# Moving the code for an expert's third to eighth token tile behind all experts

## The chip, the cores and the metric

The kernel runs on one core of one Trainium2 chip. The metric is the device time of one execution in microseconds (us); lower is better. The time before is the median of three runs.

## The reference

One layer of a diffusion backbone over 1024 latent tokens of width 1024 (and 256 context tokens), all float32: a modulated projection, neighbourhood attention beside a gated token MLP, an output projection, and then a mixture of experts. The change touches the experts alone:

```python
p_g = softmax(t @ rg_w + rg_b); p_top, g_idx = top_k(p_g, 1)          # 1 of 4 groups
e_top, e_idx = top_k(softmax(logits of that group's 4 experts), 2)     # 2 of 4 experts
gate = p_top * e_top / sum(e_top)                                      # spread to 16 columns
for e in range(16):
    hid = silu(t @ w1[e]) * (t @ w3[e])        # 1024 -> 512
    out = out + gate[:, e:e+1] * (hid @ w2[e]) # 512 -> 1024
```

Each token has two of the 16 experts, so the 16 counts of tokens add up to 2048; one expert may have anything from none to 1024 of them. The counts are known only when the program runs.

## The kernel before, in words

Projections, attention, output projection and router take the first 600 us; the router writes lists of the tokens of each expert to memory. The experts follow, in a written order (a manual schedule: every engine runs its instructions in the order of the source). Tokens of an expert are taken in tiles of 128 (`P`). A product in float32 is made of three matmuls of rounded parts (`mm3`, lines 86 to 88): high by high, high by low, low by high. Each matmul is two instructions of TensorE's stream, the load of the stationary operand (PEld in the profile) and the matmul (PE).

The weights of an expert are six chunks of 1 MB. A chunk is loaded into one of seven `raw` slots by the SP queue (`e_load`, lines 922 and 925), and is split by `e_conv` into a rounded part `chi` (ScalarE, line 941) and a rest `clo` (VectorE or GpSimd, line 946); when the rest of chunk g is made, the load of chunk g+7 is issued. So weights are loaded a little over one expert ahead.

For expert e, TensorE does the first half of the hidden columns of its first tile (`h_mm(e, 0, 0)`), then the further tiles (`more1(e)`), then the rest of the first tile: the second half (`h_mm(e, 0, 1)`), the transposes of the hidden values (`h_T`), the transposes of the next expert's first tile (`x_split`), and the second product (`y_mm`). `y_out` multiplies by gate and scatters the rows into `out` with an accumulating DMA of the GpSimd queue.

The further tiles stand under `tc.If` on `cr[e]`, the expert's count, a register that each of the five engines loads. An `If` is a compare-and-branch in the stream of each engine. `more1` (line 1521) asks whether there is a second tile at all; `second` (line 1467) takes `one` for a tile of more than 64 tokens (76 matmuls for a second tile) or `other` for a smaller one (52 matmuls, both parts in one stationary operand). Within `one` stands `more(e, 2)` (line 1504), which holds the third tile, and nested in it the fourth to the eighth. Expert 0 has only its first two tiles in place; what it has beyond them stands behind all experts (line 1583), where its weights are loaded once more.

Of the kernel before, what the change touches and what calls it, by code (L numbers as in the profile page):

```python
# [11 lines left out]
F32 = mybir.dt.float32  # L12
F32R = mybir.dt.float32r
BF16 = mybir.dt.bfloat16
I32 = mybir.dt.int32
AF = mybir.ActivationFunctionType
ALU = mybir.AluOpType
AX = mybir.AxisListType.X
# [3 lines left out]
P = 128  # L22
# [6 lines left out]
E = 16  # L29
# [10 lines left out]
def hybrid_layer_kernel(ctx, tc, a, out):  # L40
    nc = tc.nc
# [22 lines left out]
    cst = ctx.enter_context(pool("cst"))  # L64
# [22 lines left out]
        nc.tensor.matmul(po, xh, wl, start=False, stop=False)  # L87
        nc.tensor.matmul(po, xl, wh, start=False, stop=last)  # L88

# [1 line left out]
    es_p1 = ExitStack()  # L91
    p1 = es_p1.enter_context(pool("p1", side="right"))
    hp = es_p1.enter_context(pool("hp", side="right"))
# [86 lines left out]
        nc.sync.dma_start(xt, src)  # L180
        xts[t] = xt

    # rows (shift, 1 + scale) for c and c_ctx, each on all partitions
    ada = [[xp.tile([P, D], F32, name=f"ada{c}{v}") for v in range(2)] for c in range(2)]
    hT = {t: tuple(hp.tile([P, KD, P], F32R, name=f"{n}{t}") for n in ("hhi", "hlo")) for t in range(NT)}
    sqs = {}
# [62 lines left out]
            if sk == 6:  # L249
                nc.tensor.matmul(pas[j], onesr[0:2, :], bAr[j], start=False, stop=False)  # L250

    # the bias rows as a rounded part and the rest of it, on two partitions
    def bias_split():
        for v, hf in blocks:
            b = bA[:, v * D + hf * 512:v * D + hf * 512 + 512]
# [44 lines left out]
            es_w.close()  # L300
            hcp.append(es_hc.enter_context(pool("hcp", side="right")))

    # rows of a token tile where positions of a chunk come first and chunks second
    def by_pos(d, t):
        aa, b = divmod(t, 4)
        return _ap(d, (b * 256 + aa * 4) * 512, [[8 * 512, 32], [512, 4], [1, 512]])

    # rows of a token tile in the order of the keys: row group, column group, place
    def by_key(d, t, i):
        aa, b = divmod(t, 4)  # L310
        return _ap(d, (aa * 512 + b * 64) * D + i * 512, [[D, 64], [256 * D, 2], [1, 512]])
# [99 lines left out]
        return first  # L411

    def gelu_parts(t, x):
        # gelu from tanh, which is in the table set of exp
        g = gl[0]

        def p1_():
            nc.scalar.activation(g, x, AF.Square)
            nc.gpsimd.tensor_scalar(g, g, 0.044715, 1.0, op0=ALU.mult, op1=ALU.add)

        def p2_():
            nc.vector.tensor_tensor(g, g, x, op=ALU.mult)
            nc.scalar.activation(g, g, AF.Tanh, scale=math.sqrt(2.0 / math.pi))

        def p3_():
            nc.vector.scalar_tensor_tensor(g, g, 1.0, x, op0=ALU.add, op1=ALU.mult)

        m = mixt.pop(t)
        r = at0.tile([P, 1], F32, name="ru")

        def p4_():
            nc.gpsimd.tensor_scalar(g, g, 0.5, None, op0=ALU.mult)
            nc.gpsimd.tensor_tensor(g, g, m, op=ALU.mult)

        def p5_():
            nc.scalar.activation(m, g, AF.Square, accum_out=r)
            nc.gpsimd.tensor_tensor(g, g, og[1], op=ALU.mult)

        def p6_():
            rsqrt(r, r, 1.0 / 512, EPS)  # L440
            nc.gpsimd.tensor_tensor(g, g, r.to_broadcast([P, 512]), op=ALU.mult)
            nc.gpsimd.dma_start(yD[t * P:(t + 1) * P, 512:1024], g)

        def skip():
            pass
        tails.extend([p1_, p2_, p3_, p4_, skip, skip, p5_, skip, p6_])
# [38 lines left out]
            if f == 1:  # L485
                es_m.close()

    # gate and shift / scale rows of the second part, summed over the contraction on DVE
    rowD = dram.tile([4, D], F32, name="rowD")
    ada_loads = [(v, k) for v in range(4) for k in range(KD)]  # L490
    ada_raw, splits, sums = [], [], []
# [100 lines left out]
    for g, (nm, c0) in enumerate(GROUPS):  # L592
        tiles = list(range(NT))
        if nm == "v":
            tiles = tiles + [8, 9]
        if nm == "k":
            tiles = [8, 9] + tiles
        if nm == "k":
            knp.append(es_kn.enter_context(pool("knp")))
        for it, t in enumerate(tiles):  # L600
            last = it == len(tiles) - 1
# [51 lines left out]
            for k in range(KD):  # L653
# [12 lines left out]
                if k == 6:  # L666
                    if splits:
                        v = splits.pop()
# [29 lines left out]
            KS = kvp.tile([P, H, 1280], F32R, name="KS")  # L698
    es_p1.close()

# [1 line left out]
    es_o = ExitStack()  # L702
    gfp = ctx.enter_context(pool("gfp", side="right"))
    gf2 = gfp.tile([P, 2, D], F32, name="gf2")
# [5 lines left out]
    op = es_o.enter_context(pool("op", side="right"))  # L710
# [13 lines left out]
    at = es_a.enter_context(pool("at"))  # L724
# [44 lines left out]
        for lo, tr, hi in w:  # L769
            nc.vector.tensor_tensor(lo, tr, hi.bitcast(F32), op=ALU.subtract)  # L770

    # The rounded parts and the rests of v and of the weights are both side by side:
    # one pass gives all four products, which are added up on the way to o.
    def pv(t, h):
        pt = PTs.pop((t, h))
        o = psc.tile([P, 512], F32, tag="OT", name="OT").rearrange("p (a q) -> p a q", a=4)[:, 0:2]
# [113 lines left out]
    es_a0.close()  # L890
    es_kv.close()

# [1 line left out]
    g_a, sh_f, sc_f, g_f = bc  # L894
    NS, NR = 6, 7
    CH = 6 * E
# [4 lines left out]
    raw = [rawp.tile([P, 2048], F32, name=f"raw{i}") for i in range(3)]  # L901
# [4 lines left out]
    chi = [sl0.tile([P, 2048], F32R, name=f"chi{i}") for i in range(2)]  # L906
# [12 lines left out]
    def w_chunk(e, c, r, eng):  # L919
        if c < 4:  # L920
            for i, w in enumerate(("w1", "w3")):
                eng.dma_start(r.rearrange("p (k n) -> p k n", k=4)[:, :, i * 256:(i + 1) * 256],
                                  a[w][e, (c % 2) * 512:(c % 2) * 512 + 512, (c // 2) * 256:(c // 2) * 256 + 256].rearrange("(k p) n -> p k n", p=P))
        else:
            eng.dma_start(r.rearrange("p (k n) -> p k n", k=2),
                              a["w2"][e, (c - 4) * 256:(c - 4) * 256 + 256, :].rearrange("(k p) n -> p k n", p=P))
# [132 lines left out]
        nc.vector.tensor_scalar(eq, eq, f, None, op0=ALU.is_equal)  # L1059
        return m, eq  # L1060

    # one operation at a time; names mark the ends of its parts
    def route(t):
        pl = pls[t][1]
        lg = sm([P, 20], "lg")
# [28 lines left out]
        yield "pr"  # L1094
        nc.vector.tensor_tensor(msum, msum, mb, op=ALU.add)
        if t >= NT - 2:
            # places of this tile's tokens among the first tokens of expert 0
            key = sm([P, 1], "key")
            nc.vector.scalar_tensor_tensor(key, pr[:, 0:1], 1.0, mb[:, 0:1], op0=ALU.add, op1=ALU.mult)
            sel0[t] = sm([P, P], "sel0")  # L1100
            nc.vector.tensor_scalar(sel0[t], iota, key, None, op0=ALU.is_equal)
            yield "sel"
        # gates: p_top / (1 + ex) and that times ex
        ng = sm([P, 1], "ng")
        nc.vector.tensor_scalar(ng, gm, -1.0, None, op0=ALU.mult)
        nm1 = sm([P, 1], "nm1")
# [5 lines left out]
        ex = sm([P, 1], "ex")  # L1112
# [25 lines left out]
        den = sm([P, 1], "den")  # L1138
        nc.vector.scalar_tensor_tensor(den, ex, 1.0, zg, op0=ALU.add, op1=ALU.mult)
        yield  # L1140
        # the second list holds the token as a difference to the first list's row for no token
        dl = sm([P, 2, 2], "dl", I32)
        dlf = dl.bitcast(F32)
        nc.vector.reciprocal(dlf[:, 0, 1:2], den)
# [42 lines left out]
        if t + 2 < NT:  # L1187
            y_load(t + 2)

    # The first tokens of expert 0: those of all tiles but two are gathered here,  # L1190
    # those of the last two join by a product with their places.
    l0 = [cst.tile([P, 1, 2], I32, name=f"l0{i}") for i in range(2)]
    for i in range(2):
        nc.sync.dma_start(l0[i], lD[i].rearrange("(p s) c -> p s c", p=P)[:, 0:1, :])
# [76 lines left out]
    for q in range(2):  # L1271
        sl = slice(q * 4, q * 4 + 4)
        nc.scalar.activation(yT[0][0][:, sl, :], xg[q], AF.Copy)
        nc.vector.tensor_tensor(yT[0][1][:, sl, :], xg[q], yT[0][0][:, sl, :].bitcast(F32), op=ALU.subtract)
    cnt = cst.tile([P, E], I32, name="cnt")
    nc.vector.tensor_copy(cnt, pcnt[:, 0:E])
    lt = cst.tile([P, E, 8, 2], I32, name="lt")
    lt2 = rp.tile([P, E * 8, 2], I32, name="lt2")
    ltv = lt.rearrange("p e j c -> p (e j) c")
# [8 lines left out]
    es_ps2.close()  # L1288
    es_r.close()

# [1 line left out]
    # Six chunks per expert: halves of (w1 | w3) by columns, each in two halves of  # L1292
    # the contraction, and w2 in two halves of the contraction.
    ep = ctx.enter_context(pool("ep"))
    psy = ctx.enter_context(pool("psy", bufs=4, space=PSUM))
    psh = ctx.enter_context(pool("psh", bufs=2, space=PSUM))
# [10 lines left out]

    yss = {}

    # the first tile of an expert has its own banks; those of the others are shared with y  # L1310
    def bank(j, first):
        if j:
            return psy.tile([P, 512], F32, tag="y", name="yb")
# [14 lines left out]
    def gather(e, j, n=P):  # L1328
        xg = (sc_f, xgi, xg2)[min(j, 2)]
        nc.gpsimd.indirect_dma_start(out=xg[0:n, :], out_offset=None, in_=hfD[:, :],  # L1330
                                     in_offset=bass.IndirectOffsetOnAxis(ap=lt[0:n, e, j, 0:1], axis=0))
        return xg
# [51 lines left out]
        nc.gpsimd.indirect_dma_start(out=out[:, :], out_offset=bass.IndirectOffsetOnAxis(ap=lt[:, e, j, 0:1], axis=0),  # L1384
                                     in_=y, in_offset=None, compute_op=ALU.add)

    # A tile of at most 64 tokens: its rounded part and the rest of it are the two halves
    # of one stationary operand, and the two halves of the product's rows are added up.
    HP = P // 2

    def half_sum(dst, po):
# [62 lines left out]
    cr = {}  # L1454

    def count(e):
        if e < E:
            cr[e] = nc.values_load(cnt[0:1, e:e + 1], min_val=0, max_val=T)

    def gather_more(e):  # L1460
# [1 line left out]
            with tc.If(cr[e] > P):  # L1462
                gather(e, 1)

    # one of two ways through a further tile of an expert, by its number of tokens
    def second(e, j, one, other):
        with tc.If(cr[e] > P * j + HP) as c:
            one()
        with c.Else():
            other()  # L1470
# [18 lines left out]
    def more(e, j):  # L1489
        def one():  # L1490
            x_split(j)
            if j + 1 < T // P:
                with tc.If(cr[e] > P * (j + 1)):
                    gather(e, j + 1)
            h_mm(e, j, 0)
            full(e, j)
            if j + 1 < T // P:
                more(e, j + 1)

        def other():  # L1500
            half_x(j)
            half_h(e, j, 0)
            half(e, j)
        with tc.If(cr[e] > P * j):
            if j == 2:
                second(e, j, one, other)
            else:
                one()

    def more1(e):  # L1510
        def one():
            with tc.If(cr[e] > P * 2):
                gather(e, 2)
            h_mm(e, 1, 0)
            full(e, 1)
            more(e, 2)

        def other():
            half_h(e, 1, 0)
            half(e, 1)  # L1520
        with tc.If(cr[e] > P):  # L1521
            second(e, 1, one, other)
# [55 lines left out]
        y_out(e, 0)  # L1578
        conv2(g0 + 9)

    # tokens of expert 0 beyond two tiles: its weights are loaded once more
    count(0)
    with tc.If(cr[0] > 2 * P):
        for c in range(6):
            w_chunk(0, c, raw[c], nc.sync)
            nc.scalar.activation(chi[c], raw[c], AF.Copy)
            nc.vector.tensor_tensor(clo[c], raw[c], chi[c].bitcast(F32), op=ALU.subtract)
        gather(0, 2)
        more(0, 2)
    es_ms.close()  # L1590

# [86 lines left out]
```

## Time and profile before

| | us |
|---|---|
| median of the runs | 1121.88 |
| lowest and highest of the three runs | 1112.75 and 1123.05 |
| span of the profiled execution | 1111.3 |

The span goes from the first to the last instruction of one profiled execution; the profile gives that execution no other time. PE is TensorE's matmuls, PEld its weight loads, DVE VectorE, ACT ScalarE, POOL GpSimd; a "q" behind an engine's name is its sequencer, which runs branches, waits and DMA issues. Rows of a timeline read: start, duration, engine, line, operation, output and inputs, number of instructions, and in brackets the idle time of the engine before and what is taken to have ended it.

### The profile page before, as it was taken

To read this page: it belongs to the slowest core of one execution; us is meant where nothing else is said; L and a number is where in the kernel's file an instruction comes from. 1 tells how busy PE (TensorE), PEld (TensorE's weight loads), DVE (VectorE), ACT (ScalarE), POOL (GpSimd) and SP (SyncE) were. 2 spreads that over 40 slices of the span, in tenths; PEclk is the share of its full clock that TensorE was granted. 3 is DMA by queue.
4 is the path that set the end of the run, shared out by engine and by line. 5 is a ranking of instruction groups with operands and counts; after the bars stand their busy time and mean duration, and the time that the engine had idled before them with its cause. 6 is when DMAs were issued, how large, how long until landed. Compare 5 with 4: busy or idle time off the path is not lost.

```text
span 1111.3 us, 15993 instructions
## 1 busy us (share of the span) xinstructions
PE 1018.6 (92%) x5161; PEld 824.7 (74%) x5161; DVE 730.1 (66%) x1476; ACT 537.8 (48%) x1024; POOL 379.5 (34%) x311
## 2 busy tenths in 40 slices
PE   9999999999999999999998787898897989898994
PEld 4688787767879998888887665676676777686773
DVE  2777768955459998677768573667767654565722
ACT  4643243325349898642324362566556443354610
POOL 1120321232214665422235441443444333243411
PEclk9999999999999999999999998999999999999998
DMA  9784406877749879494426976799999965885512
GB/s 324 265 299 168 145 19 224 284 268 245 275 166 313 323 277 333 163 323 141 152 77 207 306 252 226 230 315 326 342 318 318 327 186 163 274 261 154 149 40 31
DMA packets 138173, 255.87 MB, mean 230 GB/s; under 512 B 10310, under 2 KB 86726, under 8 KB 137994
## 3 DMA queue, kind: packets, MB, share of 16 engines
q1 hardware_dynamic: 122876, 201.57, 53.1%
q0 software_dynamic: 15120, 52.19, 15.6%
q8 instruction: 80, 1.31, 0.5%
q14 instruction: 97, 0.79, 0.2%
HBM read 210.45 MB, written 43.29 MB: 228 GB/s over the span
## 4 chain that ended last, share of the span: by engine, by line
DMA 33%; PE 33%; issue 17%; DVE 9%; POOL 3%; ACT 2%; POOLq 1%; another core or an unknown queue 0%; SPq 0%; DVEq 0%; ACTq 0%
DMA out<-xb,lt 17%; PE po L86 6%; PE po L88 6%; PE po L87 6%; DMA gf<-hfD,lt 5%; PE OT L781 2%; DMA wraw<-in_w_ada 2%; PE pa L248 2%; DMA raw<-in_w 2%; PE tr L762 2%; DMA y<-hfD,lt 2%; DMA acc<-mixD 2%; DVE acc L504 2%; DMA bt<-in_btab 1%; POOL gf L1330 1%
## 5 line engine op out<-in xcount | busy, mean ns | idle before, releaser
L946 DVE TENSOR_TENSOR clo<-raw,chi 128x1024 fp32r<-128x1024 f32 x140 | 170.2, 1261 | 18.3 <-ACT chi L941 17.2
L941 ACT ACTIVATE chi<-raw 128x1024 fp32r<-128x1024 f32 x166 | 162.6, 1049 | 1.3 <-DMA raw<-in_w 1.3
L86 PE MATMUL po<-whi,hhi 128*128 128x512 f32 x352 | 144.8, 411 | 0.0
L86 PE MATMUL b<-chi,yhi 128*128 128x512 f32 x256 | 108.9, 425 | 34.3 <-PEq L1521 24.1
L87 PE MATMUL po<-wlo,hhi 128*128 128x512 f32 x352 | 138.9, 395 | 0.0
L88 PE MATMUL po<-whi,hlo 128*128 128x512 f32 x352 | 138.6, 394 | 0.0
L88 PE MATMUL b<-chi,ylo 128*128 128x512 f32 x256 | 105.0, 410 | 2.0 <-DVE ylo L1344 1.6
L87 PE MATMUL b<-clo,yhi 128*128 128x512 f32 x256 | 104.5, 408 | 0.0
L946 POOL TENSOR_TENSOR clo<-raw,chi 128x1024 fp32r<-128x1024 f32 x26 | 69.4, 2669 | 94.4 <-ACT chi L941 28.0
L1384 POOL DMA_INDIRECT out<-xb,lt x20 | 55.7, 2786 | 134.3 <-DVE xb L1383 92.7
L83 POOL TENSOR_TENSOR ss<-ss,nhalf 128x1 f32<-128x1 f32 (+1 forms) x36 | 44.9, 1247 | 140.4 <-DVE ss L82 140.3
L86 PEld LDWEIGHTS b<-chi,yhi 128*128 128x128 f32 x256 | 50.5, 197 | 53.6 <-ACT chi L941 23.2
L86 PEld LDWEIGHTS po<-whi,hhi 128*128 128x128 f32 x352 | 66.1, 188 | 16.1 <-issue 2.2
L88 PEld LDWEIGHTS po<-whi,hlo 128*128 128x128 f32 x352 | 66.1, 188 | 15.9 <-DVE hlo L218 0.3
L87 PEld LDWEIGHTS po<-wlo,hhi 128*128 128x128 f32 x352 | 66.3, 188 | 15.6 <-issue 2.2
L86 PE MATMUL yb<-chi,hhi 128*128 128x512 f32 x160 | 65.6, 410 | 0.0
L88 PE MATMUL yb<-chi,hlo 128*128 128x512 f32 x160 | 62.8, 393 | 0.0
L87 PE MATMUL yb<-clo,hhi 128*128 128x512 f32 x160 | 62.8, 392 | 0.0
L88 PEld LDWEIGHTS b<-chi,ylo 128*128 128x128 f32 x256 | 50.4, 197 | 14.6 <-DVE ylo L1344 2.1
L770 DVE TENSOR_TENSOR PT<-tr,PT 128x384 fp32r<-128x384 f32 (+1 forms) x128 | 56.4, 482 | 3.0 <-ACT PT L764 2.9
L87 PEld LDWEIGHTS b<-clo,yhi 128*128 128x128 f32 x256 | 50.7, 198 | 9.9
L572 DVE CUSTOM_DVE_ANT_0 S<-S,bt 128x640 f32<-128x640 f32 x64 | 52.7, 824 | 5.1 <-DMA bt<-in_btab 4.3
(314 smaller groups left out, 2359.5 us busy)
## 6 DMA issues: line engine op xcount, KB each, us to landing
raw<-in_w SPq DMA_DIRECT2D x104, 512.0 KB
raw<-in_w SPq DMA_DIRECT2D x27, 1024.0 KB
wraw<-in_w_ada SPq DMA_DIRECT2D x32, 512.0 KB
v<-vD SPq DMA_DIRECT2D x16, 768.0 KB
bt<-in_btab SPq DMA_DIRECT2D x32, 384.0 KB
wraw<-in_w_in SPq DMA_DIRECT2D x20, 512.0 KB
acc<-in_w SPq DMA_DIRECT2D x18, 512.0 KB
wada<-in_w_ada SPq DMA_DIRECT2D x16, 512.0 KB
```

What stands on the lines that cost most here:

```text
L83: nc.gpsimd.tensor_tensor(r, r, nhalf[:, :n], op=ALU.pow)
L86: nc.tensor.matmul(po, xh, wh, start=first, stop=False)
L87: nc.tensor.matmul(po, xh, wl, start=False, stop=False)
L88: nc.tensor.matmul(po, xl, wh, start=False, stop=last)
L248: nc.tensor.matmul(pas[j], sB[:, sk, :], wt[:, k, :], start=sk == 0, stop=sk == KD - 1)
L504: nc.vector.scalar_tensor_tensor(accs[v % 2], t, sT[:, k, 0:1], accs[v % 2], op0=ALU.mult, op1=ALU.add)
L572: nc.vector.tensor_tensor_reduce(sv, sv, btl[t, h // 2][:, h % 2 * 384:h % 2 * 384 + LK], op0=ALU.add, op1=ALU.max, scale=1.0, scalar=-3e3 ...
L762: nc.tensor.transpose(tr[:, i - c0, :], p[:, i * P:(i + 1) * P], ident)
L770: nc.vector.tensor_tensor(lo, tr, hi.bitcast(F32), op=ALU.subtract)
L941: nc.scalar.activation(chi[g % NS][:, sl], raw[slot_of(g)][:, sl], AF.Copy)
L946: eng.tensor_tensor(lo[:, sl], r[:, sl], hi[:, sl].bitcast(F32), op=ALU.subtract)
L1384: nc.gpsimd.indirect_dma_start(out=out[:, :], out_offset=bass.IndirectOffsetOnAxis(ap=lt[:, e, j, 0:1], axis=0), in_=y, in_offset=None, co ...
```

## The change

The code of the third to eighth tile is taken out of `more1`; it stays in place for the last expert alone, and now after the first tile's `y_out` instead of in the middle of the expert. For the other 15 experts it stands behind all experts, under one outer `If` on the largest count of experts 0 to 14 (`cr[16]`, from a new column of `cnt`) and one `If` for each expert; there the six chunks are loaded and converted again. In the third tile the small form now stands ahead of the full one.

```diff
-    cnt = cst.tile([P, E], I32, name="cnt")
-    nc.vector.tensor_copy(cnt, pcnt[:, 0:E])
+    cnt = cst.tile([P, E + 1], I32, name="cnt")
+    cmax = cst.tile([P, 1], F32, name="cmax")
+    nc.vector.tensor_copy(cnt[:, 0:E], pcnt[:, 0:E])
+    nc.vector.tensor_reduce(cmax, pcnt[:, 0:E - 1], axis=AX, op=ALU.max)
+    nc.vector.tensor_copy(cnt[:, E:E + 1], cmax)
...
     def count(e):
-        if e < E:
+        if e <= E:
             cr[e] = nc.values_load(cnt[0:1, e:e + 1], min_val=0, max_val=T)
...
         with tc.If(cr[e] > P * j):
             if j == 2:
-                second(e, j, one, other)
+                with tc.If(cr[e] < P * j + HP + 1) as c:
+                    other()
+                with c.Else():
+                    one()
             else:
                 one()
 
     def more1(e):
         def one():
-            with tc.If(cr[e] > P * 2):
-                gather(e, 2)
+            if e == E - 1:
+                with tc.If(cr[e] > P * 2):
+                    gather(e, 2)
             h_mm(e, 1, 0)
             full(e, 1)
-            more(e, 2)
...
-    count(0)
-    with tc.If(cr[0] > 2 * P):
-        for c in range(6):
-            w_chunk(0, c, raw[c], nc.sync)
-            nc.scalar.activation(chi[c], raw[c], AF.Copy)
-            nc.vector.tensor_tensor(clo[c], raw[c], chi[c].bitcast(F32), op=ALU.subtract)
-        gather(0, 2)
-        more(0, 2)
+    more(E - 1, 2)
+    with tc.If(cr[E] > 2 * P):
+        for e in range(E - 1):
+            count(e)
+            with tc.If(cr[e] > 2 * P):
+                for c in range(6):
+                    w_chunk(e, c, raw[c], nc.sync)
+                    nc.scalar.activation(chi[c], raw[c], AF.Copy)
+                    nc.vector.tensor_tensor(clo[c], raw[c], chi[c].bitcast(F32), op=ALU.subtract)
+                gather(e, 2)
+                more(e, 2)
```

The rest of the diff takes out comments.

## Rows read from the trace of the kernel before

**Rows 1.** Head of the page.
```profile
span 1111.3 us, 15993 instructions
```

**Rows 2.** Instructions of line 1521; durations are min/median/max in ns.
```profile
L1521 PEldq COMPARE_BRANCH  x15: 65/4885/8575, 642.7 to 1045.0; - x15
...
L1521 ACTq COMPARE_BRANCH  x15: 34/45/45, 647.2 to 1049.6; - x15
```

**Rows 3.** TensorE's branches of lines 1557, 1467 and 1504.
```profile
L1557 PEldq COMPARE_BRANCH  x15: 82/226/432, 636.2 to 1039.8; - x15
...
L1467 PEldq COMPARE_BRANCH  x28: 65/180/6887, 608.6 to 1084.1; - x28
...
L1504 PEldq COMPARE_BRANCH  x7: 73/2932/3637, 888.6 to 1065.4; - x7
```

**Rows 4.** Waits of PE, 600 us to end: total, times, longest.
```profile
PE b L86 <- PEq L1521: 24.1, 9, 4.9
...
PE yb L1412 <- DVE clo L946: 6.0, 2, 3.2
PE b L86 <- issue: 4.0, 2, 3.5
PE yb L1412 <- issue: 3.9, 2, 3.6
...
PE b L86 <- ACT chi L941: 2.7, 1, 2.7
PE b L86 <- PEq L1504: 1.8, 2, 1.0
```

**Rows 5.** 55 to 282 us: busy time by engine, and the instruction queue.
```profile
55.00:282.00 227.00, 222.08 (x1035) 177.44 (x1034) 162.73 (x257) 84.68 (x150) 58.87 (x61) 1.00 0.60 207
...
q8 instruction: 8, 0.13, 0.2%
```

**Rows 6.** Timeline of PE, experts 1 and 2.
```profile
653.14 0.50 PE L86 MATMUL b<-chi,yhi 128*128 128x512 f32 x1 [2.70 <-ACT chi L941]
...
679.76 0.77 PE L1412 MATMUL yb<-chi,xhi 128*128 128x512 f32 x1 [3.57 <-issue]
```

**Rows 7.** Windows of experts 4, 5 and 8, and the sum over experts 3 to 9 (PE, PEld, DVE, ACT, POOL busy; PE clock; DMA share; GB/s).
```profile
727.60:750.20 22.60, 20.06 (x86) 15.69 (x86) 15.93 (x19) 14.04 (x20) 9.70 (x5) 0.92 1.00 329
750.20:772.60 22.40, 18.72 (x86) 14.47 (x85) 15.94 (x19) 14.00 (x19) 9.58 (x4) 1.00 1.00 328
...
818.50:839.00 20.50, 18.66 (x86) 14.48 (x85) 15.94 (x19) 13.79 (x19) 7.13 (x3) 1.00 1.05 340
...
sum 160.20, PE 137.47 PEld 107.28 DVE 112.57 ACT 97.67 POOL 69.89; mean PE 19.64 PEld 15.33 DVE 16.08 ACT 13.95 POOL 9.98
```

**Rows 8.** The window of expert 2, which has a small second tile.
```profile
663.00:707.00 44.00, 36.45 (x153) 27.39 (x152) 24.36 (x33) 20.08 (x31) 11.81 (x6) 0.88 0.64 200
```

**Rows 9.** Loads of SP, transfer rates of 720 to 750 us, conversions of ACT.
```profile
719.58 13.64 SPq L922 DMA_DIRECT2D raw<-in_w  x8
...
GB/s 339 399 392 395 377 378 347 146 87 48 190 362 374 404 363 374 378 366 328 354 352 359 341 362 393 371 328 313 218 251 197 333 382 410 373 360 378 362 247 70
...
743.00 2.00 ACT L941 ACTIVATE chi<-raw 128x1024 fp32r<-128x1024 f32 x2
```

**Rows 10.** Gathers of a third tile (line 1330, into `yb`).
```profile
L1330 POOL DMA_INDIRECT yb<-hfD,lt x1: 1008/1008/1008, 1057.9 to 1057.9; - x1
```

**Rows 11.** Timeline of ACT, DVE and POOL at the end of the last expert.
```profile
1085.84 1.08 ACT L1392 ACTIVATE yb<-yb 64x512 f32<-64x512 f32 x2 [2.12 <-PE yb L1437]
...
1097.08 1.43 DVE L1383 SCALAR_TENSOR_TENSOR xb<-yb,lt,gf 128x512 f32<-128x512 f32 x2 [2.57 <-PE yb L88]
...
1089.57 1.44 POOL L1447 DMA_INDIRECT out<-xb,lt  x1 [18.41 <-DVE xb L1446]
1098.79 1.58 POOL L1384 DMA_INDIRECT out<-xb,lt  x1 [7.78 <-DVEq L1583]
```

**Rows 12.** The copy of the counts (line 1276).
```profile
L1276 DVE CAST cnt<-pcnt x1: 165/165/165, 601.1 to 601.1; 128x16 int32<-128x16 f32 x1
```

## The prediction, made before the change was run

> **What bounds the kernel now.** I read the page's head first [rows 1], then the lines of the branches that the change moves, then TensorE's waits, then windows by expert. The counts are not in the kernel, but the trace tells them: only one gather into `yb` ran, near the end [rows 10], so only the last expert has a third tile, and the code that is moved is, for 14 of the 15 experts of the loop and for expert 0, jumped over. The reader should see what a jump costs. On ScalarE it is 45 ns [rows 2]; on TensorE line 1521 has a median of 4.9 us and a maximum of 8.6, while line 1557, a jump over some 35 instructions, takes 0.23 [rows 2, 3]. From 600 us on TensorE is idle 24.1 us in nine places behind line 1521 alone, and 1.8 behind line 1504 [rows 4].
>
> Counted from the source, one matmul being two instructions, the jump of line 1521 passes 152 for `one` and 104 for `other`, and in `more` six full tiles of 168 and a small one of 120, 1128 in all: some 1,400 with waits and branches. What makes it dear is the fetch of code: between 55 and 282 us TensorE ran 1035 + 1034 instructions while the instruction queue moved 8 packets, 0.13 MB, so a packet is a page of about 260 instructions [rows 5], and that straight run hides the fetches. A jump that lands several pages ahead has to wait for its page. It has a second price: the page behind the new one is asked for only then, and when the run comes to its end too early TensorE stands again: 2.70 us in expert 1, soon after the jump's end, and 3.57 us in expert 2 [rows 6]. The profile puts the first down to a conversion on ScalarE and the second to "issue", but the operands of both were ready, and so I count four rows of [rows 4] to the jumps that don't name a branch: 6.0 (the two jumps from `one` to `other`), 4.0, 3.9 and 2.7 us. With 24.1 and 1.8 that is 42.5 us of idle TensorE. Each stall also brings the granted clock down to its lower level for a while: expert 4 has the same 86 matmuls as expert 5, at a clock of 0.92 against 1.00, and is busy 20.06 us against 18.72, so 1.34 us for such an expert [rows 7].
>
> **The change part by part.** *Jumps removed or shortened.* After it line 1521 passes some 260 instructions, one page, and the jump to `other` some 155. The trace has no jump of that length on TensorE. Below it stands 0.2 to 0.4 us (lines 1557 and the short ones of 1467), above it 2.9 to 8.6 us (lines 1504 and 1521) [rows 2, 3]. I take the lower end: the straight run shows that the next page is at hand before it is needed, so a jump into it should find it, unless the branch stands right behind a page's start. An expert now takes about 480 instructions, so the branch moves by some 30 a time against the page, and one or two of the nine meet that case.
>
> [...]
>
> *Outside the stretch of experts 3 to 10.* Idle: 6.0 + 3.9 + 2.7 + 1.8, and two of the nine of line 1521 (experts 1 and 14) at their mean of 24.1 / 9 = 2.7: together 19.8 us [rows 4]. Clock: expert 2 ran 44 us at 0.88 [rows 8], 12% or 5.3 us of cycles, of which I take 4.5 because a part fell into the stalls; experts 1, 12 and 14 at 1.34: 4.0. Sum 28.3 us. I keep back 2 us for page ends that still come too early, which the old code shows at 2.7 and 3.6 a time.
>
> *Experts 3 to 10.* Here the loads decide. Seven experts took 160.2 us, 22.9 each; at 18.7 us of full-clock matmuls and half a microsecond of small waits TensorE could do them in 7 x 19.2 = 134, a gain of 26, and the 3.5 us behind line 1504 in expert 10 come on top: 29; with one jump still missing and page ends, some 6, it is 23 [rows 4, 7]. But an expert moves about 7.4 MB (22.6 us at 329 GB/s), the DMA share is 1.00, and the best rate here is 340 GB/s: 21.8 us an expert, so 1.1 less each, 8 us in all [rows 7]. More comes only out of the lead that the loads have. The first of the eight loads issued from 719.58 have landed when the rate dips to 48 GB/s at about 727 us, and their chunk is converted at 743.0: 16 us of lead [rows 9]. TensorE can eat about 12 of them before conversions wait. The DMA thus allows some 20 us; since the lead can't be used to the end, I take 17 of TensorE's 23. What comes late next is the conversion of a chunk that has just landed. Experts 11 to 13 have two tiles each and give the DMA time to catch up.
>
> *The end.* The third tile, of 20 tokens, goes from the middle of expert 15 behind its first tile. Its matmuls and chains are the same, but its output is now the last: from the first copy of its sums to its scatter 1089.57 - 1085.84 = 3.7 us, where `y_out` takes 1098.79 - 1097.08 = 1.7 [rows 11]. That costs 2.0 us, with nothing to hide it. No weight is loaded for it, for expert 15's are still in place. The outer `If` is a long jump on all engines; it runs while the last scatter lands. If a queue had to fetch first, it would be 3 to 4 us by line 1504 [rows 3]; the landing covers it. On GpSimd the jump stands behind that scatter, on SP it delays nothing, since no load is left.
>
> *Added.* One reduction and one small copy on VectorE, each near the 165 ns of the copy of the counts [rows 12], between 0 (they wait for nothing) and 0.4 us (if the first branch waits); matmuls of expert 0 run meanwhile, and I take 0. The load of `cr[16]` takes the place of the second load of `cr[0]`: 0.
>
> Sum: 28.3 - 2 + 17 - 2 = 41 us of a span of 1111.3. The span lies 1.5 us under the fastest run and 10.6 under the median, and nothing shows where the slower runs lose theirs; I take the 41 off the median: **1081 us**, 3.7% less.
>
> **The rivals.** (a) *The DMA does not hold TensorE back*: the loads catch up in the gaps, and all 23 us or even the 29 of experts 3 to 10 come: 1069 to 1075 us. For it: the lead is 16 us, and expert 8 took only 20.5 us at 340 GB/s [rows 7]. Against it: the share of 1.00.
>
> (b) *The new jumps still miss*, because the next page isn't at hand at a branch. Then what stays is what the jumps to `other` and the ends of `one` lose (6.0 + 3.9 + 1.8 and 4.5 us of clock, the 3.5 of expert 10), less the end: about 17 us, 1104 us. For it: no jump of 260 instructions is in the trace, and the median of line 1504 is 2.9 us [rows 3].
>
> (c) *Slower*: each expert's 480 instructions end a page or two, and where the next page is asked for only after the jump has landed, TensorE stands twice in an expert, not once: the branch as before and then 2.7 to 3.6 us at the page's end as in [rows 6]. Nine times 3.1 is 28 us, less the 17 of (b): 1133 us. It decides from the point at which the next page takes longer than the matmuls that are left in the current one. Against it: in the straight run the pages come in time [rows 5].
>
> (d) *It doesn't do what it says*: an expert other than the last with a third tile would load 6 MB again, 18.5 us at 340 GB/s, with no work beside it. The gathers exclude it for this input [rows 10].
>
> **How the numbers follow.** The forecast, 1070 to 1092 by its bounds (the 17 may be 8 to 23, the page ends 0 to 6): 0.68. (a) 0.14, (b) 0.13, (c) 0.04, (d) 0.01. The range takes in (a), and of (b) the side where part of the jumps hit: 1064 to 1100. One per cent is about what a measurement of this kernel tells from no change, its runs lying 0.9% apart. Faster by over 1%: the forecast, (a) and most of (b), 0.91; within 1%: the rest of (b) and part of (c), 0.05; slower: 0.04.
>
> **What would show it.** Line 1521's branch on TensorE near 0.2 us for most experts and few waits behind it; windows of experts 3 to 9 near 20 to 21 us at first and near 22 once the lead is used up, with waits for conversions or loads in the later ones; a clock of 1.00 in experts 1, 2 and 14; in expert 2 no stall at the small tile; fewer packets on the instruction queue; a scatter of the small tile as the last one. The prediction is wrong if the branch stays at several us, if TensorE stands at page ends instead, or if experts 3 to 9 stay near 22.9 us although their branches are short.

## The result and the profile after

The changed kernel takes **1072.44 us** (median of 4 runs, 1071.03 to 1074.26); the kernel before, run beside it, 1122.47 (4 runs, 1112.75 to 1126.58). The ratio is 0.957, with an interval of 0.953 to 0.961. The profiled execution of after has a span of 1071.3 us, 40.0 less than [rows 1]. The code ahead of the experts is the same but for the two small operations on the counts, yet the experts begin at 606.3 us in it and at 599.6 in the profile of before; in other profiles with that same code ahead (second profile of the changed kernel, experiments 1 to 3, 8 and 10) they begin at 599.8 to 612.4, so this is spread and not the change. From the first expert matmul to the end it is 511.7 before and 465.1 after, 46.6 less. Steps are compared in that stretch.

The page of the kernel after, its head and the instruction queue of TensorE (packets, MB, share); before, that queue moved 80 packets in the whole run. It follows TensorE's code alone: with code added to TensorE only it moves 81 (experiment 1), with code added to the others only 60 (experiment 2):

```profile
span 1071.3 us, 15841 instructions
...
q8 instruction: 60, 0.98, 0.4%
```

The moved branch, now line 1528, and the two jumps at the end of the program (min/median/max in ns), against [rows 2]:

```profile
L1528 PEldq COMPARE_BRANCH  x15: 65/325/6158, 649.3 to 1004.9; - x15
L1528 ACTq COMPARE_BRANCH  x15: 34/45/50, 653.8 to 1009.5; - x15
L1528 DVEq COMPARE_BRANCH  x15: 43/56/63, 657.5 to 1012.5; - x15
...
L1591 POOLq EVENT_SEMAPHORE  x5: 17/43/43, 1062.8 to 1065.4; - x5
...
L1591 PEldq COMPARE_BRANCH  x1: 4742/4742/4742, 1054.1 to 1054.1; - x1
...
L1591 POOLq COMPARE_BRANCH  x1: 50/50/50, 1057.5 to 1057.5; - x1
```

TensorE's median branch fell from 4.9 us to 0.33, the maximum only from 8.6 to 6.2. Its waits from 598 us to the end (total, times, longest), against [rows 4]:

```profile
PE yb L1440 <- DVE hhi L1401: 6.4, 5, 3.5
PE b L1367 <- DVE ylo L1348: 5.1, 6, 0.9
PE b L86 <- PEq L1528: 4.1, 2, 2.5
PE yb L1429 <- DVE hB L1424: 2.0, 5, 0.7
```

The first row stands in before too, with the same 6.4 us; the last had 0.5 there. The 24.1 us behind the branch are 4.1, and of the rows that I had counted to the jumps (`clo`, two of "issue", `chi`) none is left. Windows of experts 1, 2, 4, 5, 8 and 9 after, against [rows 7, 8] (columns as there):

```profile
642.80:664.70 21.90, 18.37 (x87) 14.20 (x86) 17.18 (x22) 15.19 (x22) 11.25 (x5) 1.00 0.84 278
664.70:697.60 32.90, 31.15 (x146) 24.37 (x145) 22.96 (x31) 18.18 (x29) 11.19 (x5) 1.00 0.83 260
...
717.80:737.60 19.80, 18.64 (x86) 14.49 (x85) 17.04 (x19) 13.81 (x19) 10.31 (x5) 1.00 1.06 351
737.60:757.40 19.80, 18.68 (x86) 14.47 (x85) 17.01 (x19) 13.78 (x19) 10.64 (x5) 1.00 1.07 351
...
797.00:816.70 19.70, 18.58 (x85) 14.40 (x84) 16.93 (x18) 13.68 (x19) 10.56 (x5) 1.00 1.07 351
816.70:839.70 23.00, 20.25 (x86) 15.85 (x85) 15.92 (x18) 13.97 (x19) 11.28 (x6) 0.93 1.07 359
```

Experts 4 to 8 all take 19.7 or 19.8 us at full clock, and the rate is 351 GB/s, not 328 to 340. Expert 9 takes 23.0; in its timeline the branch's stall is seen, and the granted clock, 1.00 from 822 to 828 us, is 0.72 from 828 to 834:

```profile
828.03 0.57 PE L86 MATMUL b<-chi,yhi 128*128 128x512 f32 x1 [2.47 <-PEq L1528]
```

The periods of the experts, before and after, give the account. A period goes from TensorE's branch at the head of an expert (line 1557, now 1564) to the next one; expert 0's begins with the first expert matmul, and expert 15's goes to the end: experts 3 to 10 201.3 to 178.0 us (-23.3); expert 1 25.4 to 21.9, 2 42.1 to 32.9, 11 37.2 to 35.9, 12 37.7 to 32.9, 13 37.0 to 35.8, 14 22.8 to 19.8 (together -23.0); expert 0 36.6 to 36.5; expert 15 with the end 71.5 to 71.3.

### The profile page after: what moved, and what is told of

Same layout as the page of the kernel before. It is cut to its first block, busy times and chain, and to the rows that moved or that the text cites. A ratio compares the mean times of both kernels' runs of the same rounds, so it can differ in the third digit from the quotient of the medians.

```text
span 1071.3 us, 15841 instructions
## 1 busy us (share of the span) xinstructions
PE 1004.6 (94%) x5161; PEld 816.6 (76%) x5161; DVE 735.4 (69%) x1478; ACT 536.3 (50%) x1024; POOL 381.6 (36%) x311
## 5 line engine op out<-in xcount | busy, mean ns | idle before, releaser
L946 DVE TENSOR_TENSOR clo<-raw,chi 128x1024 fp32r<-128x1024 f32 x140 | 174.2, 1291 | 18.8 <-ACT chi L941 17.7
L1388 POOL DMA_INDIRECT out<-xb,lt x20 | 58.0, 2899 | 152.0 <-DVE xb L1387 152.0
L86 PE MATMUL b<-chi,yhi 128*128 128x512 f32 x256 | 104.7, 409 | 7.0 <-PEq L1528 4.1
L88 PE MATMUL b<-chi,ylo 128*128 128x512 f32 x256 | 101.7, 397 | 2.0 <-DVE ylo L1348 1.6
L87 PE MATMUL b<-clo,yhi 128*128 128x512 f32 x256 | 101.3, 396 | 0.0
L83 POOL TENSOR_TENSOR ss<-ss,nhalf 128x1 f32<-128x1 f32 (+1 forms) x36 | 46.0, 1276 | 144.2 <-DVE ss L82 144.0
L946 POOL TENSOR_TENSOR clo<-raw,chi 128x1024 fp32r<-128x1024 f32 x26 | 75.2, 2899 | 52.1 <-ACT chi L941 27.8
L87 PEld LDWEIGHTS b<-clo,yhi 128*128 128x128 f32 x256 | 48.5, 189 | 9.6
```

The costliest lines, as they stand in the source:

```text
L83: nc.gpsimd.tensor_tensor(r, r, nhalf[:, :n], op=ALU.pow)
L86: nc.tensor.matmul(po, xh, wh, start=first, stop=False)
L946: eng.tensor_tensor(lo[:, sl], r[:, sl], hi[:, sl].bitcast(F32), op=ALU.subtract)
```

## The experiments

Periods are read as above; "the stage" is the time from the first expert matmul to the end. In the kernels with a `pad` the added code never runs, since no expert has 1024 tokens.

**1. TensorE's jump made long again, alone.**

```diff
+    def pad(e, n):
+        with tc.If(cr[e] > T - 1):
+            po = bank(1, psy)
+            for _ in range(n):
+                nc.tensor.matmul(po[:, 0:P], onesb, onesb, start=True, stop=True)
...
     def more1(e):
         def one():
...
             full(e, 1)
+            pad(e, 588)
```

> The changed kernel with 588 matmuls of TensorE alone, never run, back in the branch of the second tile: the jump of line 1521 is some 1,445 instructions long again, as before, and no other engine gets an instruction of weight. If the gain is the length of TensorE's jumps, the branches take 4 to 8 us again and the time comes back to 1108 to 1126 us. If it is the skipped code and waits of the other engines, or the place of the third tile, it stays below 1080.

Measured: 1106.31 us (1099.02 to 1113.81), ratio to before 0.986 (0.982 to 0.990). Waits of PE and the branch, now line 1535:

```profile
PE b L86 <- PEq L1535: 18.1, 8, 4.3
...
PE b L86 <- issue: 3.9, 1, 3.9
PE yb L1416 <- issue: 2.9, 1, 2.9
PE yb L1416 <- DVE clo L946: 2.8, 1, 2.8
...
L1535 PEldq COMPARE_BRANCH  x15: 65/4698/8019, 658.2 to 1046.7; - x15
```

The length of the jump in TensorE's stream alone brings back 34 of 50 us, a little less than the 1108 us that I had named, and with it the kinds of row that name no branch: "issue" 3.9 and 2.9, and `clo` 2.8. Expert 2 takes 41.8 us again. So those rows of [rows 4] were the jumps; the fourth, `chi` in expert 1, does not come back in its place.

**2. The other engines' jumps made long, TensorE's left short.**

```diff
...
+            for _ in range(150):
+                nc.scalar.activation(pads[0], pads[0], AF.Copy)
+                nc.vector.tensor_copy(pads[1], pads[1])
+            for _ in range(60):
+                nc.gpsimd.tensor_tensor(pads[2], pads[2], pads[2], op=ALU.add)
...
```

> The changed kernel with 150 operations of ScalarE, 150 of VectorE and 60 of GpSimd, never run, in the branch of the second tile, and none of TensorE. If TensorE's jumps are the cause, the time stays at 1069 to 1077 us and the branches of these engines stay well under 1 us where their matter hides them. If skipped code costs on any engine, some 30 us or more come back: over 1100.

Measured: 1083.46 us (1082.97 to 1085.59), ratio 0.967 (0.964 to 0.970): 11 us slower than the changed kernel, which lies between the two outcomes that I had named. Waits of PE, then VectorE's timeline in expert 4, then the branch's rows:

```profile
PE b L1348 <- DVE hlo L1373: 10.3, 5, 3.4
```
```profile
729.37 1.22 DVE L949 TENSOR_TENSOR clo<-raw,chi 128x1024 fp32r<-128x1024 f32 x1
735.17 0.42 DVE L1373 TENSOR_TENSOR hlo<-b,hhi 128x256 fp32r<-128x256 f32 x1 [4.58 <-DVEq L1540]
```
```profile
L1540 PEldq COMPARE_BRANCH  x15: 65/320/4952, 647.4 to 1018.8; - x15
...
L1540 DVEq COMPARE_BRANCH  x15: 43/56/63, 656.2 to 1026.4; - x15
```

VectorE's branch has a record of 56 ns, and then the engine does nothing for 4.58 us: the wait stands behind the record. The kernel before had the same, seen only in VectorE's own waits:

```profile
DVE hlo L1366 <- DVEq L1521: 8.1, 2, 4.1
```

There TensorE stood at its own branch meanwhile, so it cost nothing more. What hides it is the very stall that the change removes.

**3. The last expert's third tile back in its middle.**

```diff
             full(e, 1)
+            if e == E - 1:
+                more(e, 2)
...
-    more(E - 1, 2)
     with tc.If(cr[E] > 2 * P):
```

> The changed kernel with the last expert's third tile back in the middle of that expert; the other 15 stay behind all experts. Prediction's term: the last output is again a full tile's, 2.0 us less, against about 1 us of TensorE idle behind the long jump over the fourth to eighth tile: 1069 to 1074 us, within 0.3% of the changed kernel. If the new place of the third tile carries part of the gain, over 1078.

Measured: 1067.70 us (1064.63 to 1070.89), ratio 0.953 (0.950 to 0.956); expert 15 with the end takes 67.8 us, not 71.3. To see this beside the changed kernel on one chip, both ran again:

> The changed kernel itself, to stand beside the others of this call: 1069 to 1074 us.

> The last expert's third tile in the middle again, now beside the changed kernel on the same chip. If the new place of that tile costs what the rows say (2.0 us at the last output, less about 1 us for the long jump behind it), this is 0 to 2 us faster than the changed kernel; if the place carries part of the gain, slower; over 3 us faster, if the prediction's price for the end was too small.

Changed kernel 1071.95 us (1065.18 to 1076.00), with the third tile in the middle 1069.55 (1064.01 to 1074.51): ratios 0.957 (0.952 to 0.961) and 0.956 (0.952 to 0.960). The times can't tell them apart, but all four profiles agree: 71.3 us in both of the changed kernel, 67.8 and 68.0 in the others. Most of the 3.4 lies behind the last scatter: from its start to the end it is 15.2 us, against 12.5 both before and with the tile in the middle. GpSimd comes to the outer `If` (line 1591) right after it, at 1057.5, and its next record comes at 1062.8, 1.4 us after the scatter has landed (1061.4); then it stands again, from 1062.9 to 1065.2.

The second stop is not the price of the tile's place. In the kernels of experiments 4 and 5 that tile is last too, and all that is added is code that never runs. In experiment 4 GpSimd's five records behind the jump (line 1595 there) lie within 0.4 us, not 2.6:

```profile
L1595 POOLq EVENT_SEMAPHORE  x5: 17/43/43, 1065.5 to 1065.9; - x5
```

In experiment 5 they lie as close. From the scatter's start to the end it is 12.6 and 12.1 us there, and expert 15 with the end takes 68.8 and 68.7. So some 2.5 of the 3.4 us hang on where the code lies, and about 1 on the tile's place.

**4. All experts' code shifted by some 96 TensorE instructions.**

```diff
+    with tc.If(cr[0] > T - 1):
+        po = bank(1, psy)
+        for _ in range(47):
+            nc.tensor.matmul(po[:, 0:P], onesb, onesb, start=True, stop=True)
     h_mm(0, 0, 0)
```

> The changed kernel with 95 instructions of TensorE, never run, ahead of the experts, so that all their code moves by 95 against the pages. [...] If the stalls come from the DMA's load at that time, the same experts stall.

Measured: 1073.75 us in one run. In the changed kernel the long branches were those of experts 3 (5.5 us), 8 (1.7) and 9 (6.2); here they are 3 (1.6), 5 (6.2) and 6 (6.1), with 0.7 in 4, and 8 and 9 are short. Nothing but the added block and, by it, the place of the code differs. The second profile of the changed kernel and those of experiments 3 and 10, where the place is the same as in it, have the three long branches where it has them (4.8 to 5.5, 1.6 to 1.7, 6.1 to 6.3). Of the three experts only 3 is long again: where the code lies sets which branches are long, by what rule no view shows.

What the trace of the changed kernel does show is when the packets of TensorE's instruction queue come. In expert 3, whose branch lasts from 702.17 to 707.68 us, one starts at 704.89 and takes 1.37 us; in expert 9 (821.71 to 827.87) one starts at 825.31 and takes 1.14; in expert 8 (801.55 to 803.23) one has started at 800.64, 0.9 us ahead of the branch, and lands 0.2 us into it. All three branches end 1.4 us after their packet has landed. In experts 1, 4 to 7 and 14, whose branches take 0.33 us, none moves during the branch, and the last one started 3.6 to 10.3 us ahead of it.

**5. Aligned branches: each expert's code made 32 TensorE instructions longer.** By the source an expert's code is some 480 instructions, with these 32 some 512, near the length of two packets of about 260 (2069 instructions to 8 packets in [rows 5]; an estimate). So the branch should come at about the same place against the packets in every expert; no view shows that place.

```diff
         def one():
...
+            pad(e, 16)
             h_mm(e, 1, 0)
...
+    with tc.If(cr[0] > T - 1):
+        po = bank(1, psy)
+        for _ in range(45):
+            nc.tensor.matmul(po[:, 0:P], onesb, onesb, start=True, stop=True)
     h_mm(0, 0, 0)
```

> The changed kernel, with 32 TensorE instructions that never run behind each expert's second tile, and a block of 90 that never runs ahead of expert 0. [...] The block ahead of expert 0 costs about 3 us of its own, so the time is that of the changed kernel or up to 3 us less: 1069 to 1073 us. Rival (the misses come from the load on the DMA at that moment, not from the place in the page): one to three branches still take 2 to 6 us, in other experts; 1072 to 1076 us.

Measured: 1076.32 us (1069.24 to 1079.18), ratio 0.959 (0.955 to 0.962). The branch, now line 1535, and the window of expert 9:

```profile
L1535 PEldq COMPARE_BRANCH  x15: 65/325/348, 657.5 to 1011.6; - x15
```
```profile
824.90:844.70 19.80, 18.63 (x85) 14.46 (x84) 17.01 (x18) 13.78 (x19) 11.62 (x6) 1.00 1.06 351
```

Not one of 15 branches takes over 0.35 us, and expert 9 takes 19.8, not 23.0: where the code lies decides whether a branch is long. The time is no better: it misses the 1069 to 1073 us and lies just above the rival's range, although the long branches that the rival named are not there. Experts 3 and 9 gained 3.6 us, but expert 0 took 41.1 us, not 36.5, with 3.1 of it in a gap at the added branch (both counted from the last matmul ahead of the experts), and expert 1 24.4, not 21.9 (it had 23.8 in the second profile of the changed kernel). Experts 10, 11 and 13, which run `one`, take 0.4 to 0.5 more each, 0.2 of it for the added branch.

**6. The next expert's split moved behind the last transpose.**

```diff
         h_mm(e, 0, 1, (2, b_hook))
+        y_mm(e, 0, 0, 1)
+        h_T(0, 1)
         if e + 1 < E:
             x_split(0)
...
-        y_mm(e, 0, 0, 1)
-        h_T(0, 1)
```

> The kernel with aligned branches, and in each expert the split of the next expert's tokens and the gather after it stand behind the last transpose of the hidden tile, not ahead of it. What TensorE still waits for in the changed kernel is mostly this: line 1367 behind VectorE's ylo, 5.1 us in six places of 0.86. Theory (TensorE, not the DMA, still sets the period of experts 3 to 9 at 19.8 us): those waits go, the periods fall to 19.0 us, and the time to 1064 to 1068 us; the loads' lead shrinks by another 0.8 us an expert and is still not used up. Rival (19.8 us is what the loads allow now): the periods stay at 19.7 to 19.8, waits for conversions of just landed chunks take the place of the ones removed, and the time stays within 2 us of the run with aligned branches alone. Second rival: the split is late for the next expert, whose first matmuls then wait 0.5 to 1 us for ylo.

Measured: 1087.82 us (1082.63 to 1096.31), ratio 0.971 (0.967 to 0.975): 11.5 us slower than experiment 5, which neither theory had. TensorE's timeline in expert 6, then its waits from 720 to 850 us:

```profile
780.96 0.44 PE L1367 MATMUL b<-ident,hA 128*128 128x128 f32 x2 [1.16 <-DVE hA L1360]
...
782.39 0.66 PE L1345 MATMUL b<-ident,gf 128*128 128x128 f32 x4 [0.56 <-DVE hlo L1370]
```
```profile
PE b L1367 <- DVE hA L1360: 6.9, 6, 1.2
PE b L1345 <- DVE hlo L1370: 3.3, 6, 0.6
```

The wait of 0.86 us was the rest of a longer one: the transposes of the split had covered the wait for `hA`. In their new place the hidden tile waits 1.16 and the split 0.56, and the periods go from 19.8 to 20.8 or 20.9 (expert 5 takes 22.4, at a granted clock of 0.93). The loads came earlier against their use by this (expert 10's second chunk has landed 14 us before it is converted, in experiment 5 7 us), so they were not what held TensorE.

**7. Both edits and the third tile in the middle.**

> The two edits before and the last expert's third tile in its old place between its tiles. Third tile alone showed 1067.7 and 1069.6 us beside 1072 for the changed kernel, a difference as large as the spread. Theory: the edits lie in different experts and add up, 1061 to 1066 us. Rival (the third tile's place is worth nothing, as the second of its runs says): the time of the run before, within 1.5 us.

Measured: 1087.55 us (1081.20 to 1096.64), ratio 0.970 (0.966 to 0.975), the time of experiment 6. Its expert 15 takes 70.7 us, so nothing is added up. Of the kernels tried none is shown to beat the changed one.

**8. All engines' jumps long again, third tile in the middle.** Experiment 1's 588 matmuls with 135 instructions each for ScalarE and VectorE and 90 for GpSimd behind the second tile of experts 1 to 14, and experiment 3's edit.

> Code of all engines, never run, back in the second tile's branch: 588 matmuls, 135 operations each of ScalarE and VectorE, 90 of GpSimd; the third tile of the last expert in the middle. If length of code is the whole effect, the experts' stage and the time come back to those of the kernel before (1110 to 1126 us), with the stalls of the engines partly hidden behind one another: less than the 34 and 11 us of the single pads over 1068 to 1072, which would give 1113 to 1117. If something else of the change matters (waits, gathers, the place of the third tile), it stays under 1100.

Measured: 1112.12 us (1107.83 to 1121.89), ratio 0.995 (0.992 to 0.998), with this wait of PE:

```profile
PE b L89 <- PEq L1546: 16.5, 8, 4.4
```

Code that never runs brings back all but some 7 us of what the change gave (the kernel before, run beside it, took 1118.88); where these 7 come from is open. Experts 4 and 8 take 19.8 us here although their branches take 4.6 and 4.5: TensorE still has matmuls queued at the branch, and they cover all but 0.7 and 0.6 us of it.

**9. A third of the experts' matmuls left out.** The low by high product is left out of the experts' tiles (but for those of at most 64 tokens, where both parts are one operand), so that TensorE's work no longer sets the period.

```diff
+    def mm2(po, xh, wh, wl, first, last):
+        nc.tensor.matmul(po, xh, wh, start=first, stop=False)
+        nc.tensor.matmul(po, xh, wl, start=False, stop=last)
...
-            mm3(po, hi[:, k, :], lo[:, k, :], wh, wl, k == 0, k == KD - 1)
+            mm2(po, hi[:, k, :], wh, wl, k == 0, k == KD - 1)
...
```

> The changed kernel with two of the three products in the experts (the low part of the tokens is left out of the sum), so that TensorE needs some 13 us for a one-tile expert. What then sets the pace of experts 3 to 9 is the rest. If the loads are limited near the prediction's 21.8 us an expert and only their lead hid it, periods go to 21 or 22 us once the lead is used, with waits for conversions and loads. If the DMA can do much more than 340 GB/s, the periods fall to 16 or 17 us, the work of VectorE.

Measured: 1039.20 us in one run. The windows of experts 4 to 6, then waits of PE from 560 us to the end:

```profile
717.30:738.10 20.80, 14.52 (x62) 10.44 (x61) 19.27 (x18) 13.87 (x19) 11.86 (x4) 0.91 1.07 351
738.10:756.50 18.40, 15.25 (x63) 11.09 (x62) 17.08 (x18) 13.77 (x19) 9.36 (x3) 0.92 1.08 346
756.50:778.50 22.00, 14.83 (x61) 11.14 (x60) 19.92 (x18) 13.92 (x20) 11.65 (x6) 0.85 1.07 359
```
```profile
PE b L1345 <- DVE hlo L1374: 20.0, 8, 5.2
PE b L1371 <- DVE hA L1364: 12.0, 8, 2.3
```

The gain comes from experts with two tiles (expert 10 28.6 us, not 35.9). Experts 3 to 9 take 20.2 us on average, though TensorE is busy only 15. VectorE, busy 91 to 93% of each window, is what TensorE waits for. Counted by the bytes of the load queue, the loads of one expert land about 21 us behind those of the one before (some 126 us from expert 4's second chunk to expert 10's, 20.8 to 21.0 for each step from expert 5 on), as in the changed kernel (some 127, and the same steps), at the same 350 GB/s, and they are still never late: their lead falls from some 15 us to 8 between those two chunks. So about 21 us is what the DMA gives an expert here, and 7 experts are too few to use the lead up.

**10. The path that this input never takes.**

```diff
-    with tc.If(cr[E] > 2 * P):
+    with tc.If(cr[E] > P + HP):
         for e in range(E - 1):
             count(e)
-            with tc.If(cr[e] > 2 * P):
+            with tc.If(cr[e] > P + HP):
```

> The changed kernel, with the moved block entered by experts with more than 192 tokens, not 256: experts 10, 11 and 13 load their 6 MB a second time, convert them and gather a tile, and compute nothing, since no third tile is there. It is the price of the path that this input never takes, without its matmuls. First theory (a reload costs its transfer, as in rival (d) of the prediction): 6 MB at 340 GB/s are 18.5 us an expert; the first one's loads run while expert 15 computes, and its 6 conversions on VectorE take 2.8 us each, 17 us; 17 + 2 x 18.5 + some 3 = 57 us, so 1125 to 1135 us. Second theory (the skips count too): the branches over the block of each expert that is not reloaded are far jumps on all engines, over some 1,200 instructions on TensorE, and ten of them stand ahead of expert 10; at the 3.3 to 5.5 us that far jumps took so far these are 33 to 55 us more before VectorE and ScalarE come to the first conversion: 1160 to 1185 us.

Measured: 1173.89 us (1170.89 to 1174.15), ratio 1.047 (1.043 to 1.050): 101 us more than the changed kernel, as the second theory had it. The branches in the block, then ScalarE's and SP's timeline:

```profile
L1594 SPq COMPARE_BRANCH  x16: 38/45/58, 993.2 to 1163.5; - x16
...
L1594 PEldq COMPARE_BRANCH  x16: 70/4429/7485, 1052.1 to 1140.2; - x16
L1594 ACTq COMPARE_BRANCH  x16: 38/45/50, 1051.1 to 1168.8; - x16
L1594 DVEq COMPARE_BRANCH  x16: 47/56/63, 1053.3 to 1169.1; - x16
```
```profile
1108.72 9.11 ACT L1597 ACTIVATE chi<-raw 128x2048 fp32r<-128x2048 f32 x5 [57.79 <-PEq L1594]
```
```profile
1084.74 8.40 SPq L922 DMA_DIRECT2D raw<-in_w  x8
```

Ten skips keep TensorE from 1052.1 to 1108.5 us, and ScalarE's first conversion waits for TensorE to be through, though ScalarE has passed its own ten by 1082.3 and SP issues the first loads from 1084.74 on. Three reloads then take 63.2 us to the end, 21 each. So a single expert with a third tile would pay the skips of others too, over and above the 18.5 us of rival (d); that case itself was not run.

## Why the prediction was right, point by point

**The bound.** That TensorE waits for its own code is shown by experiments 1 and 8: code that is only jumped over costs 34 us alone on TensorE, and on all engines all but some 7 us of the gain. In the trace of before one or two packets of its instruction queue start in each of the nine branches of line 1521 that take over 4 us, and one in each of the two stalls of [rows 6], at 650.67 and 677.23; when a packet is asked for, no view shows. Three of the four rows without a branch's name come back with it (experiment 1), so I had counted them rightly. "Each stall also brings the granted clock down" was wrong: expert 5, which I took for one without a stall, stood longer behind its branch than expert 4, and its clock stayed at 1.00.

```profile
738.69 0.47 PE L86 MATMUL b<-chi,yhi 128*128 128x512 f32 x1 [2.39 <-PEq L1521]
...
761.87 0.47 PE L86 MATMUL b<-chi,yhi 128*128 128x512 f32 x1 [3.03 <-PEq L1521]
```

The price of 1.34 us is that of expert 4, whose granted clock was 0.72 for the 6 us behind its stall; it does not hold for every stall.

**Jumps of one page.** I took 0.2 to 0.4 us with one or two of nine missing: the median is 0.33, and three of experts 3 to 9 miss, two of them fully. "Unless the branch stands right behind a page's start" is not shown, since no view gives a branch's place in a page. Shown is a packet that lands during each of the three long branches and during none of the short ones of experts 1, 4 to 7 and 14 (experiment 4).

**Outside experts 3 to 10.** 28.3 less 2 was forecast, 23.0 came. Expert 12 gave 4.8, about as summed. Expert 2 gave 9.2 where 10.9 stood (2.8 and 3.6 of idle, 4.5 of clock). Experts 1 and 14 were mis-sized: at a mean of 2.7 us a jump, a page end and 1.34 us of clock I had 6.7 and 4.0, they gave 3.5 and 3.0. Experts 11 and 13 gave 1.3 and 1.2, for the 1.8 behind line 1504. In expert 1 the branch of 4.3 us had cost TensorE only 0.5, since matmuls already queued covered the rest: a mean over nine places hid this. No row of a page's end is left in the new code's experts, so the 2 us kept back were not needed.

**Experts 3 to 10.** This is the step that was off most: 17 forecast, 23.3 measured, and that is rival (a)'s price for it. TensorE's 23 came out in the sum, in part by luck: experts 3 to 9 gave 18.1 where 20 stood (26 less 6), their period being 19.8 rather than 19.2 (0.86 us of it the new wait for `ylo`), and expert 10 gave 5.2 where 3.5 stood, as a wait of 1.3 us for VectorE's `xlo` went too. The discount for the DMA was wrong in its rate: 340 GB/s, the best of a window in which TensorE stood still at times, was not the limit. It gives 351, so about 21 us an expert, not 21.8; 7 x 1.9 = 13 us, and the rest of the 18.1 that experts 3 to 9 gained came out of the lead, some 15.5 us in expert 4 and 8.5 in expert 9 (second chunks). It was never used up: between 676 and 835 us ScalarE, which reads a chunk first, waited for none. What came late next was the 0.86 us, not the loads.

**The end.** -2.0 forecast; expert 15 with the end came out 0.2 shorter than before, for the jumps that went there too. Against the same kernel with the tile in the middle it is 3.4 in the profiles, 2.4 to 4.7 in the medians, and only about 1 of it is the tile's place (experiment 3). "The landing covers it" is the part that failed: GpSimd's first stop at the outer `If` ended 1.4 us after the landing, and a second one of 2.3 us followed, which is bad luck of where the code lies.

**Added.** 0 was taken for the two operations on the counts, and expert 0 went from 36.6 to 36.5.

**The other engines.** "On ScalarE it is 45 ns" read the record and not the engine. The sum did not suffer, for this cost was hidden before, and no wait of TensorE shows it after; experiment 2 gives its price once TensorE is quick: 11 us.

**The sum.** 28.3 - 2 + 17 - 2 = 41 against 46.6 in the stage: +6.3 in experts 3 to 10, +2.3 at the end with expert 0, -3.3 outside. The medians differ by 50.0; the remaining 3.4 us are not in these two profiles. The bounds were added up wrongly: the 17 at 23 and at 8 with the page ends at 0 and at 6 give 1073 to 1094, not 1070 to 1092. So 1072.4 lies at the edge of the forecast and is the time of rival (a), 1069 to 1075, to which I had given 0.14; the range held because it took (a) in.

## What to carry to other kernels

Look for code that is skipped far more often than it is run: the length of a jump is a cost of its own (here 34 us for the same work, with some 1,445 instructions of TensorE passed and not 260), and it shows only in part under the branch's name. Read what an engine does behind a far branch, not how long the branch's record is (VectorE in experiment 2: 56 ns of record, then 4.58 us of nothing), and count the stall of the slowest engine as cover for all the others. Moving rare code away makes the usual case fast and the rare one dear, here by 101 us for three experts without their matmuls; say for which input the trade is made.

## What the hardware showed that was not expected

- Of branches over some 260 to 300 instructions of TensorE most take 0.33 us and a few 1.7 to 6.2 us, by where the code lies: in the changed kernel those of experts 3, 8 and 9 (5.5, 1.7 and 6.2), with 96 instructions more ahead 3, 5 and 6 (1.6, 6.2 and 6.1), with 32 more in each expert none (15 of 15 within 0.35). Each of the three of the changed kernel ends 1.4 us after an instruction packet has landed in it.
- On VectorE and ScalarE the wait is not in the branch's record (56 and 45 ns) but in the silence behind it: up to 4.6 us on VectorE in experiment 2, 1.9 us on ScalarE behind line 1521 before. On TensorE it is in the record.
- Behind a far jump a second stop can follow: GpSimd stood until 1062.8 and again to 1065.2 at the end of the changed kernel, alike in its second profile, and only once in experiments 4 and 5.
- The conversions on line 946 slow down as the experts run closer: a VectorE one from a `raw` slot took 1261 ns on average before, 1291 after and 1417 in experiment 9, a GpSimd one 2669, 2899 and 3133. Those clear of any GpSimd one take 1219 ns on average before and 1220 after; six after that run wholly beside GpSimd ones take 2482 to 2521 (before, the one such took 1211).
